# A sliding-window copy: twelve staged batches in 32 KB packets instead of eleven in 16 KB packets

## The chip, the cores and the metric

The kernel runs on one core of one Trainium2 chip. Times are device microseconds of that core, medians of several executions. Nearly all of the work is done by the core's 16 DMA engines, which copy between the main memory (HBM) and the on-chip memory (SBUF), or within HBM; the compute engines only issue transfers. Ratios compare runs of the same chip and the same rounds.

## The reference

The reference cuts each of 32 batches of 4096 rows of 256 float32 into 127 windows of 64 rows, 32 rows apart:

```python
batch, length, dim = (32, 4096, 256)
window_size, stride = 64, 32
for i in range(n_windows):                 # 127
    start = i * stride
    result[:, i] = x[:, start:start + window_size].copy()
```

A block of 32 rows is 32 KB. A window is two neighbouring blocks (64 KB), so every inner block is written twice: as the second half of one window and the first half of the next. The input is 134 MB, the output 266 MB.

## The kernel before

A batch is copied in one of two ways. A direct batch goes from HBM to HBM: each window is read and written, 8.3 MB read and 8.3 MB written. A staged batch is loaded once into an SBUF tile of 128 blocks (4.2 MB) and stored from there twice, once as the first halves and once as the second halves. It reads only 4.2 MB of HBM, but the DMA engines move 4.2 + 8.4 = 12.6 MB for it, where a direct batch moves 8.3 MB.

Three queues run side by side. The scalar engine's queue (q10) issues loads and stores of the staged batches in two groups: loads of six tiles, stores of six, loads of five, stores of five. The sync engine's queue (q1) issues the direct copies. The GpSimd queue (q0) issues the remainders at the end: 127 windows are seven times 16 plus 15, and the 15 next to a staged batch have to wait until that batch is stored, since its stores spill over the edge.

```python
DIRECT, IN, OUT = 32768, 16384, 16384        # bytes of a packet

def windows(self, q, b, w0, n, half=None, piece=DIRECT):     # direct: n windows, whole or one half
    blk = self.blk
    row = [1, 2 * blk if half is None else blk]
    h = half or 0
    return q.dma_start(
        out=self.oap((b * self.nw + w0) * 2 + h, [[2 * blk, n], row]),
        in_=self.xap(b * self.nb + w0 + h, [[blk, n], row]),
        max_dma_last_dim=piece,
    )
# ... Staging:
    parts = [(k, 4, 32, 1) for k in range(4)] if g == 0 else [(0, step, n, step)]   # loads: one DMA a tile
    parts, end = [((0, step, n, step), 0), ((0, step, n, step), 1)], []             # stores: one DMA a half
# ... kernel:
    staged = [*range(1, B, 3)]                                # 11 batches
    share += 120 if turns < 16 or -8 <= second < 16 else 90 if loading else 18
    if share >= 120:                                          # 16 windows as two half-window DMAs
        count(c.windows(ring_d, b, w, 16, 0), done)
        count(c.windows(ring_d, b, w, 16, 1), sem)
    else:                                                     # or as one whole-window DMA
        count(c.windows(ring_d, b, w, 16), sem)
# ... remainders, in groups of 15 windows, on the GpSimd queue:
    ring_r.wait_ge(near, 16)
    for b, w, n in edges:
        ...
        count(c.windows(ring_r, b, w, n), rest)
```

Each DMA on q1 and q10 ends, on every engine that it uses, with a 4-byte semaphore packet, which tells that the data has landed (q1: 204 DMAs, 3264 such packets). In the packet records of the stores (150 to 400 us) the queue changes from one packet of an engine to the next in 99% of the cases, whether data or semaphore packet: the queues take turns, and the semaphore packet takes a turn too. So the number of data packets per semaphore packet in a queue sets how the engine's time is divided. I call the part of the moved bytes that belongs to direct copies (q1 and q0) the direct share.

## Time and profile before

751.6 us (751.08 to 752.81). The page of the kernel before: busy DMA engines in 40 slices, what they moved, and its share by queue.

```profile
span 749.4 us, 322 instructions
DMA  8999999999999999999999999999999999999996
GB/s 360 401 427 429 427 429 428 434 423 418 420 424 423 418 424 415 422 427 427 414 427 417 429 432 429 430 422 430 429 423 421 423 421 419 425 426 423 431 409 262
DMA packets 18290, 313.26 MB, mean 418 GB/s; under 512 B 4336, under 2 KB 4336, under 8 KB 4528
q1 hardware_dynamic: 8016, 154.32, 48.8%
q10 hardware_dynamic: 9104, 138.41, 44.0%
q0 software_dynamic: 1168, 20.51, 6.5%
HBM read 220.95 MB, written 267.09 MB: 651 GB/s over the span
```

The engines are busy from start to end, so every us of this kernel is on the critical path: the chain of waits says nothing more here. The 4336 smallest packets are the semaphore packets.

The stretches view of the kernel before, in the first load phase, first store phase, second load phase, second store phase and the phase of the remainders. Columns: stretch, length, GpSimd busy with its instructions, clock, DMA share, GB/s.

```profile
40.00:125.00 85.00, 0.00 (x0) 1.00 1.01 428
150.00:400.00 250.00, 0.00 (x0) 1.00 1.00 422
420.00:505.00 85.00, 0.00 (x0) 1.00 1.00 429
530.00:650.00 120.00, 0.00 (x0) 1.00 1.01 422
670.00:735.00 65.00, 2.30 (x4) 1.00 1.00 418
```

The rate differs by phase although the engines are never idle. A busy engine is therefore not always at its best; packets take longer in some phases.

The DMA issues of the kernel before (count, KB each, median us from issue to landing) show the forms: whole-window direct DMAs of 1 MB, half-window ones of 512 KB, stores and loads of 4 MB, and remainders of 15 windows.

```profile
out_dram<-in_x_dram SPq DMA_DIRECT2D x92, 1024.0 KB, 100.7
out_dram<-xb ACTq DMA_DIRECT2D x21, 4096.0 KB, 139.7
out_dram<-in_x_dram SPq DMA_DIRECT2D x110, 512.0 KB, 90.3
xb<-in_x_dram ACTq DMA_DIRECT2D x10, 4096.0 KB, 131.4
out_dram<-in_x_dram POOLq DMA_DIRECT2D x20, 960.0 KB, 38.5
```

The trace holds a record of each packet. At best a 32 KB packet takes 1213 ns, a 16 KB packet 611, a 4 KB packet 159 and a semaphore packet 9 (a few records are 2 or 3 ns shorter). Three words follow from these and are used below:

- the floor of a kernel is the sum of the best durations of all its packets over 16 engines;
- the stretch is what the recorded durations have above the floor, in us per engine or in ns per 32 KB (not to be taken for the stretches view, which is the profile's table of pieces of time);
- the lag is how long, on average, an engine has ended its last packet before the last engine ends.

These three are read from one profiled execution of each kernel, while the times are medians; the profiled one can be the fastest of its runs (even12) or the slowest (eleven3).

### The profile page before, as it was taken

What the parts mean: (1) busy time and instruction counts of PE and PEld (TensorE: products, weight loads), DVE (VectorE), ACT (ScalarE), POOL (GpSimd) and SP (SyncE); (2) the same over time, 40 slices, a digit from 0 to 9 for tenths busy, and PEclk for the clock granted to TensorE, in tenths of its full rate; (3) what the DMA queues carried; (4) which work ended last, traced back from release to release, by engine and by line L of the source; (5) the groups of instructions that cost most, each with busy time, mean ns of one, the idle gap of its engine ahead of it and who ended that gap; (6) DMA issues with size and microseconds to landing.
All of it is one profiled execution on the core that took longest, in us unless ns stands there. A gap on an engine that the chain in (4) does not pass through costs nothing.

```text
span 749.4 us, 322 instructions
## 1 busy us (share of the span) xinstructions
POOL 12.8 (2%) x26
## 2 busy tenths in 40 slices
POOL 0000000000000000000000000000000000040100
DMA  8999999999999999999999999999999999999996
GB/s 360 401 427 429 427 429 428 434 423 418 420 424 423 418 424 415 422 427 427 414 427 417 429 432 429 430 422 430 429 423 421 423 421 419 425 426 423 431 409 262
DMA packets 18290, 313.26 MB, mean 418 GB/s; under 512 B 4336, under 2 KB 4336, under 8 KB 4528
## 3 DMA queue, kind: packets, MB, share of 16 engines
q1 hardware_dynamic: 8016, 154.32, 48.8%
q10 hardware_dynamic: 9104, 138.41, 44.0%
q0 software_dynamic: 1168, 20.51, 6.5%
q14 instruction: 2, 0.02, 0.0%
HBM read 220.95 MB, written 267.09 MB: 651 GB/s over the span
## 4 chain that ended last, share of the span: by engine, by line
another core or an unknown queue 92%; POOL 2%; issue 0%; POOLq 0%; SPq 0%
POOL out_dram L34 2%; POOL out_dram L44 0%; POOLq L236 0%; SPq L172 0%; POOLq L114 0%
## 5 line engine op out<-in xcount | busy, mean ns | idle before, releaser
L34 POOL DMA_DIRECT2D out_dram<-in_x_dram x21 | 12.0, 576 | 691.3 <-DMA out_dram<-in_x_dram 654.0
L44 POOL DMA_DIRECT2D out_dram<-in_x_dram x1 | 0.6, 581 | 0.0
L222 POOL MEMSET const-float32-0.0<- 128x1 f32 x1 | 0.1, 98 | 0.2 <-issue 0.2
L222 POOL MEMSET const-bfloat16-1.0<- 128x1 bf16 x1 | 0.1, 101 | 0.0
L222 POOL MEMSET const-float32-1.0<- 128x1 f32 x1 | 0.1, 98 | 0.0
L222 POOL MEMSET const-uint8-127<- 128x1 uint8 x1 | 0.1, 98 | 0.0
## 6 DMA issues: line engine op xcount, KB each, us to landing
out_dram<-in_x_dram SPq DMA_DIRECT2D x92, 1024.0 KB, 100.7
out_dram<-xb ACTq DMA_DIRECT2D x21, 4096.0 KB, 139.7
out_dram<-in_x_dram SPq DMA_DIRECT2D x110, 512.0 KB, 90.3
xb<-in_x_dram ACTq DMA_DIRECT2D x10, 4096.0 KB, 131.4
out_dram<-in_x_dram POOLq DMA_DIRECT2D x20, 960.0 KB, 38.5
xb<-in_x_dram ACTq DMA_DIRECT2D x4, 1024.0 KB, 15.7
out_dram<-xb ACTq DMA_DIRECT2D x2, 1024.0 KB, 113.4
out_dram<-xb ACTq DMA_DIRECT2D x4, 512.0 KB, 96.9
```

Source lines behind the costliest of these rows:

```text
L34: return q.dma_start(out=self.oap((b * self.nw + w0) * 2 + h, [[2 * blk, n], row]), in_=self.xap(b * self.nb + w0 + h, [[blk, n], row]), m ...
L44: return q.dma_start(out=self.oap((b * self.nw + w0) * 2, [[part, 16], [2 * self.blk, n], row]), in_=self.xap(b * self.nb + w0, [[part, 16 ...
L222: nc = _bacc.Bacc("TRN2", target_bir_lowering=False, num_devices=1)
```

## The change

The intent: stage one batch more, which takes load from HBM; move the staged bytes in 32 KB packets like the direct ones, which saves the fixed part of half of the packets; cut loads and stores into as many DMAs as give the wanted direct share; and issue the direct copies in large half-window DMAs with seven packets per engine. The remainders stay last.

```diff
-DIRECT, IN, OUT = 32768, 16384, 16384
+DIRECT, IN, OUT, REST = 32768, 32768, 32768, 32768
+    def many(self, q, b, w0, n, half):
+        return q.dma_start(
+            out=self.oap((b * self.nw + w0) * 2 + half, [[2 * self.blk, 16], [32 * self.blk, n], [1, self.blk]]),
+            in_=self.xap(b * self.nb + w0 + half, [[self.blk, 16], [16 * self.blk, n], [1, self.blk]]),
+        )
 # Staging.load
-        parts = [(k, 4, 32, 1) for k in range(4)] if g == 0 else [(0, step, n, step)]
+        for rows in self.split(2 if g < 6 else 3):
+    def split(self, parts):
+        if parts == 3:
+            return [(0, 4, 32, 1), (2, 4, 32, 1), (1, 2, 64, 1)]
+        return [(k, parts, 128 // parts, 1) for k in range(parts)]
 # Staging.store
+        split = self.split(4 if g >= len(self.items) - 2 else 3)
+        parts, end = [(rows, half) for half in (0, 1) for rows in split], []
 # kernel
-    staged = [*range(1, B, 3)]
+    staged = [0, 3, 6, 9, 11, 14, 17, 20, 22, 25, 28, 31]
+        main += [(b, w + 16 * j, min(7, 7 - j), half) for j in range(0, 7, 7) for half in (0, 1)]
+            edges += [(b, 0, 8), (b, 120, 7)]          # a direct batch between two staged ones
+            edges.append((b, 0 if before else 112, 15))
-        for i, (b, w) in enumerate(sixteens):
-            ...
+        for i, (b, w, n, half) in enumerate(main):
+            count(c.many(ring_d, b, w, n, half), near if i == len(main) - 2 else done)
```

More of the change, by code (lines that the diff above doesn't have):

```diff
@@ L37, in windows, with quarters @@
             max_dma_last_dim=piece,
+        )
+    def quarters(self, q, b, w0, p0, n):
+        part = self.blk // 4
+        at = p0 * 2 * part
+        dims = [[n * part, 2], [1, n * part]]
+        return q.dma_start(
+            out=bass.AP(self.out.tensor, self.oap((b * self.nw + w0) * 2, dims).offset + at, [[2 * self.blk, 4], *dims]),
+            in_=bass.AP(self.x.tensor, self.xap(b * self.nb + w0, dims).offset + at, [[self.blk, 4], *dims]),
+            max_dma_last_dim=4 * n * part,
+        )
+    def many(self, q, b, w0, n, half):
+        return q.dma_start(
+            out=self.oap((b * self.nw + w0) * 2 + half, [[2 * self.blk, 16], [32 * self.blk, n], [1, self.blk]]),
+            in_=self.xap(b * self.nb + w0 + half, [[self.blk, 16], [16 * self.blk, n], [1, self.blk]]),
         )
@@ L87, in load @@
         i = g % len(self.tiles)
-        b, c, n = self.items[g]
         if self.count[self.stored[i]]:
             q.wait_ge(self.stored[i], self.count[self.stored[i]])
-        step = 128 // n
-        parts = [(k, 4, 32, 1) for k in range(4)] if g == 0 else [(0, step, n, step)]
-        for rows in parts:
-            self.issue(self.c.load(q, self.tiles[i], b, c, rows), self.loaded[i])
+        for rows in self.split(2 if g < 6 else 3):
+            self.issue(self.c.load(q, self.tiles[i], *self.items[g], rows), self.loaded[i])
         self.after_load[g] = self.count[self.loaded[i]]
+    def split(self, parts):
+        if parts == 3:
+            return [(0, 4, 32, 1), (2, 4, 32, 1), (1, 2, 64, 1)]
+        return [(k, parts, 128 // parts, 1) for k in range(parts)]
     def store(self, q, g):
         i = g % len(self.tiles)
-        b, c, n = self.items[g]
         q.wait_ge(self.loaded[i], self.after_load[g])
-        step = 128 // n
-        parts, end = [((0, step, n, step), 0), ((0, step, n, step), 1)], []
+        split = self.split(4 if g >= len(self.items) - 2 else 3)
+        parts, end = [(rows, half) for half in (0, 1) for rows in split], []
         if g == len(self.items) - 1:
-            parts = [((0, 1, 128, 1), 1), ((0, 1, 32, 1), 0)]
-            end = [(96, 1, 32, 1)] + [(32 + k, 4, 16, 1) for k in range(4)]
+            parts = [(rows, 1) for rows in split] + [(split[0], 0)]
+            end = split[1:]
         for rows, half in parts:
-            self.issue(self.c.store(q, self.tiles[i], b, c, rows, half), self.stored[i])
+            self.issue(self.c.store(q, self.tiles[i], *self.items[g], rows, half), self.stored[i])
         for rows in end:
-            self.issue(self.c.store(q, self.tiles[i], b, c, rows, 0), self.ended)
+            self.issue(self.c.store(q, self.tiles[i], *self.items[g], rows, 0), self.ended)
         self.after_store[g] = self.count[self.stored[i]]
@@ L140 @@
     c = Copier(x, out, B, L, D, W, S, n_win)
-    staged = [*range(1, B, 3)]
-    items = [(b, -1 if b == B - 1 else 0, c.nb) for b in staged]
-    place = {b: g for g, (b, _, n) in enumerate(items) if n == c.nb}
+    staged = [0, 3, 6, 9, 11, 14, 17, 20, 22, 25, 28, 31]
+    items = [(b, 1 if b == 0 else -1 if b == B - 1 else 0) for b in staged]
+    place = {b: g for g, b in enumerate(staged)}
     direct = [b for b in range(B) if b not in staged]
@@ L157, in count @@
         total[sem] += 16
-    sixteens = []
+    main, edges, singles = [], [], [(B - 1, c.nw - 1, 1)]
+    if 0 in staged:
+        singles.append((0, 0, 0))
+    last = B - 2
     for b in direct:
-        w = 15 if b - 1 in staged else 0
-        sixteens += [(b, w + 16 * j) for j in range((c.nw - w) // 16)]
-    singles = [(B - 1, c.nw - 1, 1)]
-    edges = [(b, 0 if b - 1 in staged else 112, 15) for b in direct[:-1]]
-    last = B - 2
-    edges.append((last, 112, 4))
-    first_loads, loads, stores = 6 * 17, 5 * 17, 6 * 34
-    turns = share = 0
+        before, behind = b - 1 in staged, b + 1 in staged
+        w = 15 if before and (not behind or b == last) else 8 if before else 0
+        if b == last:
+            w = 0
+        main += [(b, w + 16 * j, min(7, 7 - j), half) for j in range(0, 7, 7) for half in (0, 1)]
+        if b == last:
+            edges.append((b, 112, 13))
+        elif before and behind:
+            edges += [(b, 0, 8), (b, 120, 7)]
+        else:
+            edges.append((b, 0 if before else 112, 15))
+    b, w, n, half = main.pop()
+    main += [(b, w, n - 1, half), (b, w + 16 * (n - 1), 1, half)]
     with tc.tile_critical():
         st.run(ring_s)
-        for i, (b, w) in enumerate(sixteens):
-            sem = near if i == len(sixteens) - 2 else done
-            second = turns - first_loads - stores
-            loading = turns < first_loads or 0 <= second < loads
-            share += 120 if turns < 16 or -8 <= second < 16 else 90 if loading else 18
-            if share >= 120:
-                share -= 120
-                turns += 4
-                count(c.windows(ring_d, b, w, 16, 0), done)
-                count(c.windows(ring_d, b, w, 16, 1), sem)
-            else:
-                turns += 3
-                count(c.windows(ring_d, b, w, 16), sem)
-            if i == len(sixteens) // 2:
+        for i, (b, w, n, half) in enumerate(main):
+            count(c.many(ring_d, b, w, n, half), near if i == len(main) - 2 else done)
+            if i == len(main) // 2:
                 for b, w, half in singles:
@@ L196 @@
                     st.wait_stored(ring_r, place[k])
-            count(c.windows(ring_r, b, w, n), rest)
-        count(c.columns(ring_r, last, 116, 9), rest)
+            count(c.windows(ring_r, b, w, n, None, REST), rest)
         st.wait_stored(ring_d, place[B - 1])
```

## The prediction

> **What bounds it now.** Nothing computes; 16 DMA engines copy. The page's slices show DMA at 9 tenths from slice 2 to 39, mean 418 GB/s; part 3 gives q1, q10 and q0 together 99.3% of the engines' time. The stretches view gives 428 to 430 GB/s in the load phases (us 40 to 130 and 425 to 505) and 421 to 423 in the store phases (160 to 285, 300 to 400, 520 to 645), 401 in us 20 to 40, and a falling tail after 740.
>
> From the trace's packet records: a 32 KB packet takes 1213 ns at best and 1236 on average; two 16 KB packets take 1222 at best and 1249 on average; a 4-byte semaphore packet takes 9 ns. The best packet means 432 GB/s over 16 engines, near the 435 of the Trainium skill ("DMA: Bandwidth & Descriptors", Where 436 GB/s comes from). So packet rate is the floor. Above it lies about 17 us of stretched packets, mostly in store phases: 5-us pieces with a direct share (bytes) near 0.59 have 1245 to 1250 ns per 32 KB, near 0.51 only 1220 to 1230. HBM traffic there is about 660 GB/s, so I take the stretch for HBM pressure: a direct packet touches HBM twice, a staged one once.
>
> **What changes.** 11 staged batches become 12. A direct batch moves 8.3 MB through the engines, a staged one 12.5 MB, so DMA bytes rise from 313.3 to about 317 MB: +7 to 8 us at the best rate (plus 1%). HBM traffic falls from 488 to about 484 MB (minus 1%). Staged packets of 32 KB instead of 16 KB save 9 ns per 32 KB (2.4 us per engine), and semaphore packets fall from 271 to about 170 per engine (1 us). The two rings alternate packet by packet (the skill, same page, Queues, rings and completion order; the shares in the trace fit it), so turns set the direct share: 7/8 against 4/5 makes .522 in loads, against 8/11 makes .546 in stores, where before has about .53 and .57.
>
> **The sum.** Floor by an alternating-ring count: before 728 us, after about 734.5. Stretch: before 17; after, loads 1, the start 3, stores at .546 about 1% of 490 us, 5: 9. Ends: 5 us idle plus 2 us between span and time, unchanged. 734.5 + 9 + 7 = 750; if all-half windows also lower the stretch, 746. The direct ring should finish some 10 us before the staged one, which then runs alone at full rate: no loss.
>
> All of it is critical, since the engines never idle; the larger byte count and the smaller stretch nearly cancel.
>
> **Prediction: 748.5 us, 8 in 10 between 742.5 and 755. Faster by over 2%: 0.02, within 2%: 0.95, slower: 0.03.** Faster by 2% means 736.6 us, below the floor plus the ends.
>
> **What would show each step.** DMA bytes about 317 MB, HBM about 217 MB read. Store phases at 425 to 430 GB/s instead of 422, load phases at 430 to 431. q1 with q0 ending before q10. If stores stay at 422 the share was not the cause of the stretch and the time is 755 or more; if they reach 431, 745.
>
> **What would make it wrong.** The stretch belongs to the store's access pattern, not to the HBM sum; the rings drift out of balance, leaving direct packets alone at the end; the windows on the GpSimd ring (298 instead of 304, no multiple of 16) or the final two-window copy leave engines uneven, a few us.

## The result

761.79 us (760.36 to 765.83, 6 runs) against 752.35 us (751.08 to 752.89, 6 runs) on the same chip: ratio 1.0137, 95% interval 1.011 to 1.0163. A ratio is the mean time of one kernel's runs over that of the other's runs of the same rounds, so it is not quite the ratio of the medians. Executions over 1.5% slower than the fastest of the same kernel are left out of the means. The change made the kernel 1.4% slower, and the time lies outside the predicted range of 742.5 to 755.

The page of the changed kernel:

```profile
span 760.1 us, 231 instructions
DMA  8999999999999999999999999999999999999995
GB/s 364 431 421 428 433 426 419 431 433 422 431 421 431 426 428 426 424 431 431 421 402 433 421 421 426 422 417 433 419 428 424 422 428 428 429 410 407 416 405 241
DMA packets 12609, 317.54 MB, mean 418 GB/s; under 512 B 2860, under 2 KB 2860, under 8 KB 2924
q10 hardware_dynamic: 6304, 151.00, 47.2%
q1 hardware_dynamic: 5248, 147.00, 45.6%
q0 software_dynamic: 1056, 19.53, 6.3%
HBM read 216.86 MB, written 267.19 MB: 637 GB/s over the span
```

The bytes are as predicted (317.5 MB through the engines, 216.9 MB read). The mean rate has not moved: 418 GB/s before and after. So 1.4% more bytes took 1.4% more time.

The stretches view of the changed kernel, in its five phases:

```profile
40.00:120.00 80.00, 0.00 (x0) 1.00 1.01 428
140.00:370.00 230.00, 0.00 (x0) 1.00 1.00 427
390.00:505.00 115.00, 0.00 (x0) 1.00 1.00 423
530.00:640.00 110.00, 0.00 (x0) 1.00 1.00 425
670.00:740.00 70.00, 2.88 (x5) 1.00 1.00 408
```

The stores did get faster, from 422 to 427 and 425 GB/s. But the second load phase fell from 429 to 423, and the phase of the remainders from 418 to 408. The DMA issues of the changed kernel show the new forms; note that 18 loads are of 2 MB and 12 of 1 MB, the latter from the second group, which is cut in three:

```profile
out_dram<-in_x_dram SPq DMA_DIRECT2D x39, 3584.0 KB, 167.4
out_dram<-xb ACTq DMA_DIRECT2D x56, 1024.0 KB, 140.1
xb<-in_x_dram ACTq DMA_DIRECT2D x18, 2048.0 KB, 94.5
out_dram<-in_x_dram POOLq DMA_DIRECT2D x17, 960.0 KB, 45.4
xb<-in_x_dram ACTq DMA_DIRECT2D x12, 1024.0 KB, 144.5
```

The packet records give an account that adds up to the span (us per engine; the phases are cut where the staged bytes of each group end, and where the first remainder starts):

```
                                   before   after
floor (best durations)              729.6   736.3
overlap of neighbouring packets      -4.0    -2.5
stretch                              15.0    16.6
   first loads   (direct share)       3.0     3.0     (.537 / .517)
   first stores                       6.3     3.4     (.572 / .539)
   second loads                       0.7     3.7     (.525 / .547)
   second stores, until remainders    2.8     2.1     (.560 / .519)
   remainders                         2.2     4.5     (.584 / .475)
lag at the end                        2.7     3.8
start, last landing                   6.2     5.9
span                                749.4   760.1
```

The overlap row was news to me: with the records of one engine put in a chain (a record does not name its engine, so the chains are inferred from the times), each packet starts about 3.6 ns before the end of the one ahead of it. So, by this reckoning, a saved packet saves 3.6 ns less than its record says.

Of the difference of 10.7 us, 6.7 are the floor, 1.5 the overlap, 1.6 the stretch and 1.1 the lag. The relief of HBM did come in the stores (3.6 us less stretch in both store phases together), but the second loads gave back 3.0 us and the remainders 2.3. Packets that took less than 150 ns too long fell from 9.4 us to 4.9; those that took 300 ns and more too long rose from 78 packets (2.3 us) to 226 (8.3 us).

### The profile page after: what moved, and what is told of

It is laid out like the page before. It is cut to its first block, busy times and chain, and to the rows that moved or that the text cites. A ratio compares the mean times of both kernels' runs of the same rounds, so it can differ in the third digit from the quotient of the medians.

```text
span 760.1 us, 231 instructions
## 1 busy us (share of the span) xinstructions
POOL 12.9 (2%) x26
## 4 chain that ended last, share of the span: by engine, by line
another core or an unknown queue 93%; POOL 2%; issue 0%; POOLq 0%; SPq 0%
POOL out_dram L34 2%; POOLq L252 0%; SPq L201 0%; POOLq L134 0%
```

## The experiments

### First four: the loads, the last stores, eleven batches, and the layouts by themselves

Theory A is that the cut of the staged DMAs into strided rows stalls packets. Its rivals are the direct share, and the remainders.

load2way: `for rows in self.split(2 if g < 6 else 3)` becomes `for rows in self.split(2)`.

> The changed kernel with one edit: the second group of loads is issued in two DMAs per tile like the first, not in three. In the changed kernel the second load phase lost 3.65 us per engine to stretched packets, of which most in packets that took over 300 ns too long; the kernel before lost 0.67 us there. Theory A (the three-way split of the loads causes the long stalls): the second load phase falls to about 1 us of stretch and the time by about 3 us, to 758 to 759. Rival B (the direct share of .547 in this phase, or the addresses met at that time): with B by share, it falls too, since the share goes to .522; with B by addresses or by the transition itself, the stalls stay at over 2.5 us and the time stays at 761 to 762.

Measured: 761.0 us, ratio 1.0106 (1.0082 to 1.013). The stretch of the second loads fell from 3.65 us to 1.30, at a share of .525. The total stretch fell only by 1.0 us, since more direct work was left for the end: 4.85 us of stretch in the remainders and a lag of 4.6 us. The local effect came out as expected; this run does not tell the cut from the share.

tail3: `split = self.split(4 if g >= len(self.items) - 2 else 3)` becomes `split = self.split(3)`.

> The changed kernel with one edit: the last two tiles are stored in three DMAs per half, not in four. The changed kernel lost 4.5 us per engine to stretched packets in the phase of the remainders, plus 4 us of engines ending unevenly. Theory A (the store split in DMAs of two rows per engine stalls): stretch in that phase falls to about 2.5 us, time 2 us lower at most, since the staged ring then also ends earlier and leaves the remainders alone. Rival B (the remainders on the GpSimd ring cause the stalls whatever the split): no change within 1 us, or slower by 1 to 2 us because the staged share rises and the remainders end later.

Measured: 762.19 us, ratio 1.0129 (1.0111 to 1.0148); stretch in the remainders 4.6 us. The cut of the last stores is not the cause there: rival B.

eleven: the staged list of before, its remainders, loads in two and three DMAs, stores in four, in the second group eight:

```diff
-    staged = [0, 3, 6, 9, 11, 14, 17, 20, 22, 25, 28, 31]
+    staged = [*range(1, B, 3)]
-        split = self.split(4 if g >= len(self.items) - 2 else 3)
+        split = self.split(4 if g < 6 else 8)
```

> The changed kernel's packets and direct DMAs (32 KB, 7 windows halves per engine and DMA), but with the eleven staged batches of before and its last remainders, and more splits (loads 2 and 3 DMAs, stores 4, then 8) so that the direct share stays at what eleven batches need. Theory A (the twelfth batch is what costs: 4.2 MB more through the engines, floor 6.7 us higher): the floor is about 726 us, the stretch like before's 15 us or less, the time 747 to 751, so at or under the kernel before. Rival B (the new packets and DMAs cost by themselves): 755 or more.

Measured: 765.18 us, ratio 1.0171 (1.0149 to 1.0194). The floor was 726.8 us as expected, but the stretch 27.3 us, of which 11.5 in the second stores, where stores in eight let the direct share rise to .61. I had missed the share, so this run tells only that too high a share is costly.

layouts: Its output is wrong, which doesn't matter for the time. It runs loads, then stores, in 1, 2, 3 and 4 DMAs per tile with barriers between, first alone and then beside direct DMAs, then stores beside remainders:

```python
for kind, parts, n, other, m in PHASES:       # e.g. ('load', 3, 4, 'many', 5)
    for i in range(n): ...                    # n tiles, each in `parts` DMAs, on the scalar queue
    for j in range(m): ...                    # m direct DMAs on the sync queue, or remainders on GpSimd
    barrier()
```

> A kernel that is wrong on purpose: 21 phases with barriers between them. Each of 1, 2, 3 and 4 DMAs per tile, for loads and for stores, first alone, then beside direct DMAs; then stores in 1, 3 and 4 beside 15-window remainders from GpSimd; then direct DMAs alone and remainders alone. Read from the packet records: mean excess over 1213 ns of each phase. Theory A (layout): three- and four-way splits show long stalls (mean excess over 40 ns) even alone, one- and two-way under 15. Rival B (meeting of streams): no split stalls alone; all splits alike beside direct packets, 10 to 30 ns. Rival C (remainders): the stalls come only in the phases with remainders and even where these run alone.

Measured, over 50 us in the middle of each phase, with the direct share and the sum of HBM bytes read and written per second:

```
                          GB/s   share   HBM GB/s   stretch per 32 KB
loads alone, 1 to 4 DMAs                             0 ns
stores alone, 1 to 4 DMAs                            5 to 7 ns
loads  1 + direct         432.5  .500    649         2 ns
loads  2 + direct         428.3  .510    647        14 ns
loads  3 + direct         418.8  .549    649        40 ns
loads  4 + direct         412.0  .577    650        61 ns
stores 1 + direct         431.5  .506    650         5 ns
stores 2 + direct         430.1  .516    652         7 ns
stores 3 + direct         426.8  .557    665        18 ns
stores 4 + direct         420.4  .574    662        36 ns
stores 1 + remainders     414.6  .407    583        53 ns
stores 3 + remainders     419.4  .455    610        36 ns
stores 4 + remainders     419.2  .488    624        35 ns
direct alone              327.3 1.000    655       390 ns
```

Two lines of the stretches view of this kernel, direct DMAs alone and 15-window remainders alone, show the limit without any arithmetic: the engines stay busy, but the rate is 320 and 326 GB/s.

```profile
1114.00:1144.00 30.00, 0.00 (x0) 1.00 0.98 320
1161.00:1191.00 30.00, 0.00 (x0) 1.00 1.02 326
```

No cut stalls alone, so theory A in its plain form falls. So does rival B, which had all cuts alike: beside direct DMAs the stretch grows with the share, and the HBM sum stays at 647 to 665 GB/s whatever the cut. The exception is the remainders: 35 to 53 ns at HBM sums of only 583 to 624, uncut stores included.

### Share against number of DMAs, and which ring makes the remainders stall

streams: Its output is wrong, which doesn't matter for the time. Loads in four DMAs meet direct DMAs of two packets per engine, which lowers the share to about .49; unsplit loads in 16 KB packets meet direct DMAs of seven packets, which raises it to .65.

> A kernel that is wrong on purpose: 16 phases with barriers. Theory H (the stretch is set by the direct share alone, through HBM: rate = about 657 GB/s over 1 plus the direct share, or the engines' 432 GB/s, whichever is less): loads in four DMAs beside direct DMAs of two packets per engine (share .50) show under 10 ns of mean excess, although four-way loads showed 50 ns at share .577; one-DMA loads in 16 KB packets beside direct DMAs of seven packets (share about .64) fall to about 400 GB/s although they are not split; stores in four beside pairs (.50) under 20 ns. Rival S (the number of splits or DMAs sets it): the four-way phases keep 40 ns and more, the one-DMA phase stays at 425 GB/s or more. Remainders: if the GpSimd ring is the cause of the late stalls, full 16-window DMAs from GpSimd beside three-way stores stall (over 40 ns) and the same from the sync ring do not (under 20 ns); if it is the 15 of 16 engines, only the 15-window ones do; if it is the whole 64 KB windows, both rings do and the half-window ones do not. Direct alone: all near 330 GB/s; if whole windows save HBM effort over half windows, they are some per cent faster alone, and stores in 16 KB packets beside whole windows beat those beside half-window pairs.

Measured, in the stretches view of this kernel (four-DMA loads at a share of .485, then unsplit loads at .648):

```profile
12.00:62.00 50.00, 0.00 (x0) 1.00 1.00 431
97.00:147.00 50.00, 0.00 (x0) 1.00 1.01 400
```

The four-DMA loads have 2.7 ns of stretch where they had 61 at .577, four-DMA stores 1.2; the unsplit loads fall to 400 GB/s at an HBM sum of 657. Theory H holds and rival S falls. (This chip is a faster one than that of layouts: before takes 744.75 us on it. So 61 against 2.7 is not of one chip; four-DMA loads at full rate against unsplit loads at 400 GB/s is.) Half windows and whole windows are equally fast alone (331 GB/s each). The phases on the GpSimd ring issued no direct DMA, by a mistake in my kernel, and were repeated:

streams2: the same, with whole windows in DMAs of 16 or 15, from GpSimd and from the sync ring, beside three-DMA stores.

> Wrong on purpose: the phases for the remainders again (in the earlier trial those from the GpSimd ring issued nothing, by a mistake of mine). Stores in three DMAs of 32 KB packets beside whole windows. If the GpSimd ring causes the long stalls: 16-window DMAs from GpSimd give over 30 ns of mean excess, from the sync ring under 5 (the earlier trial: 1.6). If the 15 of 16 engines cause it: only the 15-window ones, from GpSimd and from the sync ring alike, exceed 30 ns. Half-window pairs from the sync ring repeat about 20. With 16 KB store packets beside 15-window remainders from GpSimd: if packet size matters, few packets over 300 ns too long, at HBM traffic of 658 GB/s; if not, as many as with 32 KB.

Measured, in the stretches view: 16 windows from GpSimd, 15 from GpSimd, 15 from the sync ring, 16 from the sync ring.

```profile
34.00:84.00 50.00, 0.00 (x0) 1.00 1.01 433
123.00:173.00 50.00, 0.00 (x0) 1.00 1.00 417
298.00:348.00 50.00, 0.00 (x0) 1.00 0.99 419
387.00:437.00 50.00, 0.00 (x0) 1.00 1.01 435
```

In the packet records of the same stretches: 0.8 ns of stretch with 16 windows from GpSimd, 40.5 with 15; from the sync ring 1.4 with 16, 14.9 with 15. The long stalls (300 ns and more) number 0, 32, 15 and 0. The ring alone is not the cause, since 16 windows run undisturbed from both; the count of 15 windows is. The ring matters for the size: I had expected over 30 ns from both, and the sync ring has half of that, which no run explains. The Trainium skill ("DMA: Bandwidth & Descriptors", Why a DMA increments its semaphore by 16 and not by 1) says that a DMA runs on the largest number of engines up to 16 that divides its outer dimension, so 15 windows run on 15 (with an exception for some copies from GpSimd); from the sync ring the chains of packet records agree: in these 50 us one engine has 3 direct packets, the others 17 to 20. From GpSimd all sixteen have 18 or 19, so there no engine stays without direct work for long, and the stall is not a matter of lasting uneven load. How 15 windows stall the engines is not shown. Two more readings: beside loads, 15 windows cost nothing (0.0 ns), and beside stores in 16 KB packets, 15 and 16 windows stretch alike (47 and 51 ns over a slightly longer stretch, at shares of .57 and .59, where the HBM limit is reached). So the 15 windows are seen to matter only beside stores in 32 KB packets; with 16 KB packets the HBM limit may hide what they add. Each phase of stores beside direct DMAs also begins with some 24 to 48 packets stalled by over 150 ns in its first 10 us, whatever the DMAs, and then runs nearly without any where all engines get the same work and the share is under .5; I read this as the engines falling into step, which an uneven DMA breaks again. That reading is argued, not shown.

### Putting the finds into the kernel

eleven2 takes eleven batches with shares nearer to before's; even12 keeps twelve and evens the share out.

```diff
 # eleven2: loads split(2), stores split(4), the last three tiles in 16 KB packets
+        piece = OUT if g < 8 else OUT // 2
 # even12: loads split(2)
+        split = self.split(1 if g >= 9 else 3 if g % 2 else 2)
+        piece = OUT if g < 9 else OUT // 2
```

> Eleven staged batches again, with 32 KB packets and seven-half direct DMAs, but now with the direct shares that the kernel before had: loads in two DMAs, stores in four (about .57), the last three tiles in four DMAs of 16 KB packets beside the remainders (about .58). The first trial with eleven failed since its stores in eight had a share of .61 and ran into the HBM limit (11 us of stretch in one phase). Theory A (the twelfth batch and the uneven shares are what costs, the packets are a small gain): floor 727 us, stretch 13 to 16, time 747 to 752, the same as the kernel before or 0.5% under it. Rival B (32 KB packets or half-window direct DMAs cost by themselves): 755 or more.

Measured: 760.31 us where the kernel before took 755.62 on this chip; ratio 1.0068 (1.0035 to 1.0102). The stretch was 24.9 us. In the second stores the share was .59 again, since the 16 KB tiles came up while the main part still ran. A miss, by my own sizing.

> The changed kernel with twelve batches but the direct share held nearer to one value: loads in two DMAs (.522), stores in three and two by turns (about .535), the last three tiles unsplit in 16 KB packets so that the remainders get about .54 instead of .475. Theory A (the loss lies in shares over .53 in loads and stores and in the remainders beside 32 KB stores): stretch falls from 16.6 to about 11 us, the uneven end from 4 to 3, the time to 752 to 756. Rival B (the remainders' long stalls stay whatever the staged packets): stretch in that phase stays over 4 us and the time at 757 or more.

Measured: 759.73 us, ratio 1.006 (1.0029 to 1.0092), less than half of the changed kernel's loss, though that was measured on another chip. The stretch fell to 11.4 us, with 1.3 in the remainders (share .52, stores in 16 KB packets) and 1.4 in the second loads; the lag was 2.5 us. The stretch and the lag came out as theory A said, the median 4 us over its range, on a chip where before itself was 3 us slower. The profiled execution (755.45 us) was the fastest of the four; what the others lost above it no trace shows.

### One chip for all: before, after, even remainders, and the best of twelve

> The kernel before, for a profile on the same chip as the next three runs, since the trials showed that chips differ in what their HBM gives. Expected: 15 us of stretched packets per engine if this chip is like the first one, over 18 if its time is over 755.

Measured: 744.02 us, stretch 7.6 us (a single look, so its state is unknown; the seven timed runs of before on this chip have a median of 744.6). This chip has half of the stretch of the first one with the same kernel.

> The changed kernel once more, for the same reason and for the ratio to before on this chip. Expected ratio 1.01 to 1.016, 16 to 18 us of stretch, over 4 us of it in the phase of the remainders.

Measured: 756.48 us, ratio 1.0159 (1.0134 to 1.0184), stretch 9.0 us. My expectation for the stretch was taken from the slower chip and missed, but the account of the difference is the same: floor 6.7, stretch 1.5, overlap 1.5, lag 0.4 us.

edge16 issues the remainders as 16 windows, one of them written a second time after the first write has landed:

```diff
-            edges += [(b, 0, 8), (b, 120, 7)]
+            edges += [(b, 0, 16), (b, 111, 16)]      # with 96 windows, not 112, in the main part of such a batch
-            edges.append((b, 0 if before else 112, 15))
+            edges.append((b, 0 if before else 111, 16))
+        ring_r.wait_ge(body, total[body])            # all main DMAs but the last two
```

> The changed kernel, with its remainders in DMAs of 16 windows, not 15, 8 or 7, so that all 16 engines get the same work: one window is written twice, after the first write has landed, with the same bytes (1.3 MB more, about 2.9 us of floor). Theory (remainders on 15 of 16 engines beside stores cause the long stalls; seen in the trials with barriers: 35 to 47 ns of mean excess against 1 to 2): stretch in that phase falls from 4.5 to under 2 us and the uneven end from 4 to about 3; the time is 0 to 3 us lower in spite of the added bytes. Rival (something else in that phase, such as the store split or the waits of GpSimd): stretch stays over 4 us and the time rises by 3 us.

Measured: 754.07 us, ratio 1.0122 (1.0105 to 1.0139), 2.4 us less than the changed kernel although the floor is 2.8 us higher. This gain is not clear of the noise: the two intervals overlap, and of the two profiled executions edge16's is 1.0 us the slower. The stretch in the remainders fell from 3.3 us to 0.5, and the packets there that took 300 ns and more too long from 65 to 13; even12, with 15 windows beside stores in 16 KB packets, has 1. The stretches view of the remainders in the changed kernel on this chip:

```profile
660.00:735.00 75.00, 2.88 (x5) 1.00 1.00 414
```

The same view of edge16:

```profile
650.00:735.00 85.00, 2.57 (x5) 1.00 1.00 431
```

With streams2 this makes 15-window DMAs beside 32 KB stores the cause of most of the long stalls in the remainders. The lag did not fall (4.9 us), which the theory had got wrong.

best12 adds loads in two DMAs, stores in three and two by turns, and the last three tiles in four.

> The 16-window remainders together with loads in two DMAs throughout and stores in three and two by turns, the last three tiles in four: the direct share is held at .50 to .535 everywhere. If the three terms found (share over .53 in the loads, share in the stores, remainders on 15 engines) are the whole of the loss beyond the bytes, stretch falls to 8 to 10 us; floor 739; time 1.000 to 1.006 of before, so a tie and no gain, because the twelfth batch and the doubled windows cost 10 us of floor.

Measured: 754.95 us, ratio 1.0145 (1.0124 to 1.0165). The stretch was 5.9 us, and in the second loads 0.1: the stretches view has them at the engines' best.

```profile
380.00:485.00 105.00, 0.00 (x0) 1.00 1.00 433
```

But the expected tie did not come. On this chip before loses only 7.6 us to stretch, so there were not 10 us to win; the floor of 739.0 us decides. The remainders on q0 also ended 9 us after the staged queue.

### Do the packets and the direct DMAs cost anything by themselves?

eleven3: eleven batches, loads in three, stores in four, only the last two tiles in 16 KB packets; before_third is the kernel before on the same chip.

> The kernel before, for its profile on the chip of the next run: floor 729.6 us, stretch between 7 and 19 us, as its time on this chip tells.

> Eleven staged batches with 32 KB packets and half-window direct DMAs, now with loads in three (.546) and stores in four (.567) and only the last two tiles in 16 KB packets, so that the share stays under .57 while the main part runs (the second trial had .59 there). If the new packets and DMAs cost nothing by themselves: floor 727 us, stretch within 2 us of before's on this chip, ratio to before .995 to 1.004. If they cost by themselves: stretch over 4 us above before's and ratio over 1.006.

Measured: before 753.56 us with 17.2 us of stretch; eleven3 761.78 us, ratio 1.0072 (1.0041 to 1.0103), with 28.4 us of stretch. The floor was 726.8 us. At first loads of equal share (.54) it had 4.9 us against 2.8, and in the second stores, at .541 against .560, 6.0 against 3.4. Part of the gap in stretch is the choice of executions (eleven3's profiled one is the slowest of its four, before's single one is at the fast end), but the ratio is over 1 although the floor is 2.8 us lower. So something does cost by itself, and the share is not the whole law. Two runs take the parts one by one.

before32 is the kernel before with 32 KB staged packets, in eight DMAs per tile so that a turn still moves 16 KB on average; halfpairs is the kernel before with most whole-window direct DMAs replaced by pairs of half-window ones.

```diff
 # before32
-DIRECT, IN, OUT = 32768, 16384, 16384
+DIRECT, IN, OUT = 32768, 32768, 32768
+        parts = [(k, 8, 16, 1) for k in range(8)]        # loads; stores likewise
-            share += 120 if ... else 90 if loading else 18
+            share += 120 if ... else 65 if loading else 0
 # halfpairs, for two neighbouring groups of 16 windows
-                count(c.windows(ring_d, b, w, 16), sem)
+                    count(c.many(ring_d, b, w - 16, 2, 0), done)
+                    count(c.many(ring_d, b, w - 16, 2, 1), done)
```

> The kernel before with one thing changed: the staged packets are 32 KB, in DMAs of one packet per engine (eight per tile), so that the staged ring's turn moves 16 KB on average as it did with 16 KB packets, and the direct share stays about the same (.57 in stores; the mixture of direct DMAs is shifted a little to keep it). Eleven batches, whole windows, remainders as before. If the 32 KB staged packets by themselves bring the long stalls that the third trial with eleven batches showed: stretch over 5 us above before's 17 on such a chip, and a ratio over 1.005. If the packets are innocent: floor 2 us lower, stretch about the same, ratio .994 to 1.002.

> The kernel before with one thing changed: most whole-window direct DMAs (two 32 KB packets of one window per engine) become pairs of half-window DMAs (two packets of two windows 16 apart), with the same count of packets and turns, so the same shares. Staged packets stay at 16 KB. If half-window direct DMAs cost by themselves (a block is read again only later): stretch over 5 us above before's and a ratio over 1.005. If they are innocent: ratio .997 to 1.003.

Measured: halfpairs 745.89 us, ratio 1.0012 (0.9996 to 1.0029), so half-window DMAs in pairs are innocent; in sevens they were not tried alone. before32 gave 765 to 790 us in four runs, where before gave 745.3; two of the four count as slow, so no ratio is drawn from it. The stretches view of its profiled (fast) run, in the first loads and the first stores:

```profile
10.00:90.00 80.00, 0.00 (x0) 1.00 1.00 340
150.00:400.00 250.00, 0.00 (x0) 1.00 1.01 428
```

Its stores, in eight DMAs of 32 KB packets, ran as fast as before's on a chip of like speed (before_again, 150 to 400 us: 428 GB/s too), and as fast as those of halfpairs on the same chip (426 there, and 425 against 424 in the second stores). So 32 KB packets in stores are innocent at this share. Its remainders are not: 15 windows beside 32 KB stores, 73 packets stalled by 300 ns and more, where halfpairs with 16 KB stores has 1. Its first loads stalled for 20.9 us per engine, at a share of .527 and an HBM sum of 510 to 535 GB/s, and recovered after 100 us by themselves. Loads that are finely cut can stall for a reason that is not the HBM sum.

load3share asks this of the changed kernel itself: the three-DMA loads stay, and the direct DMAs that meet them are cut in two, which lowers the share.

```diff
+    main = [(b, w + 16 * a, k, half) for i, (b, w, n, half) in enumerate(main)
+            for a, k in (((0, 4), (4, 3)) if 23 <= i < 32 else ((0, 7),))]
```

> The changed kernel again, for its profile on the chip of the next run. Second load phase at a share of .547: 1.6 us of stretch on a fast chip (as in after_again), 3.6 on a slow one.

> The changed kernel with its three-DMA loads kept, but the direct DMAs that meet the second group of loads cut in two (four packets and three per engine, so 7 data packets in 9 turns), which takes the direct share there from .547 to about .517, as far down as the two-DMA loads took it. If the share sets the stretch of the loads: the second load phase falls to under half of the control's (1.3 us or less where the control has 3.6; 0.8 or less where it has 1.6). If the splitting of the loads sets it, as before32's 21 us in its first load phase suggests: it stays within 30% of the control's.

Measured: the control after_third took 757.7 us, with 2.0 us of stretch in the second loads at .547; load3share has 0.4 us there at .501. The stretches view of the second loads in the control:

```profile
390.00:505.00 115.00, 0.00 (x0) 1.00 1.00 429
```

The same view of load3share:

```profile
390.00:490.00 100.00, 0.00 (x0) 1.00 1.01 433
```

So in the changed kernel it was the share, not the cut of the loads (one profile each; the direct DMAs were also shorter). The time did not follow: 758.35 us, ratio 1.015 (1.0093 to 1.0207; the four runs spread from 751.8 to 761.0). What the direct queue did not move in the second loads had to be moved later: the remainders began at 654 us, not 648, and finished 9 us after the staged queue (3 in the control), with a lag of 8.1 us.

No version beat the kernel before.

## Why the prediction was wrong

The prediction said 748.5 us; 761.8 was measured. Its sum was 734.5 of floor, 9 of stretch and 7 of ends. Measured: 736.3, 16.6 and 9.0 (overlap, lag, start and landing, and the 1.8 us between span and time). The headline of 748.5 was also 1.5 us under its own sum, for a hope that half windows would lower the stretch; halfpairs shows that they don't.

- "DMA bytes rise ... plus 7 to 8 us at the best rate", with a floor from 728 to 734.5: right. The floor rose by 6.7 us, and that is most of the loss. The level was 1.8 us too low.
- "Staged packets of 32 KB instead of 16 KB save 9 ns per 32 KB": too high. Because neighbouring packets overlap by 3.6 ns, a saved packet is worth about 5.4 ns. This is the 1.5 us in the overlap row.
- "Stores at .546 about 1% of 490 us, 5": right until the remainders began. Both store phases together had 5.5 us. In mid-phase (530 to 640 us) the share was .545 as forecast. That the stretch follows the direct share, with a nearly constant HBM sum, was shown by layouts and streams, and for the loads by load3share; eleven3 shows that the share is not all.
- "After, loads 1, the start 3": here a step failed. I took ".522 in loads" for all loads. The second group is cut in three, and by the same count of turns that makes .546, which was measured as .547. These loads had 3.7 us where before had 0.7. With the two-DMA cut it was 1.3, and with the three-DMA cut at a share of .501 it was 0.4 against 2.0 for the control.
- The remainders had no term of their own. I had only listed uneven engines as a risk of "a few us". They took 4.5 us of stretch at an HBM sum of about 600 GB/s, where the share law allows none, because 15-window DMAs beside 32 KB stores stall; with 16 windows 0.5 us remained of 3.3.
- "The direct ring should finish some 10 us before the staged one": it did not. The remainders on q0 ended at 756.7 us, the staged queue at 754.0 (before: 745.8 and 745.2).
- "Ends: ... unchanged": the lag grew by 1.1 us on the first chip. How much of this belongs to the 15 windows is open: edge16 did not lower it.
- "Stores ... if they reach 431, 745; if they stay at 422 ... 755 or more": they reached 425 to 427, and the time was still over 755. The store rate was not the only test that this sum needed.

So the step that failed is the stretch term: predicted to fall from 17 to 9 us, it went from 15.0 to 16.6. HBM relief did what it should in the stores, and 3.6 us of it were given back as 5.3 us in the second loads and the remainders. That left the added bytes unpaid.

Two things stay open. Why eleven3 stretches more than the kernel before at nearly equal shares: half windows in pairs and 32 KB stores were cleared one by one, but not their combination, nor half windows in sevens, nor the cut of the loads at shares over .53. And why the first loads of before32 stalled for 100 us and then recovered.

## What to carry to other kernels

Where a kernel trades bytes through the DMA engines against bytes through HBM, write one sum for each of the two limits and for each phase: a phase pays the larger one, and a good average share does not help a phase that is over the limit. Whatever share is taken out of one phase comes back in another, most often at the end, so look there first when a local gain doesn't reach the time. And give every DMA an outer count that is a multiple of 16: uneven DMAs cost nothing beside loads here, but 15 to 40 ns on each 1213 ns packet beside stores in 32 KB packets.

## What the Trainium skill lacked or had wrong

- "DMA: Bandwidth & Descriptors", Where 436 GB/s comes from: its 435 GB/s agrees (432 by the best packet). Under Latency and other measured facts the page has copies between HBM tensors at up to 214 GB/s per direction; direct copies here moved more, 319 to 331 GB/s, so 638 to 662 GB/s read and written together, and a mixed load is held to about 650 to 671. "HBM Reference", Specifications, sees a core streaming alone as bounded by its 16 engines at about 425; direct copies alone stay far below that, at about the HBM sum at which mixed loads stop too, so I take HBM for their bound.
- "DMA: Bandwidth & Descriptors", Queues, rings and completion order: turns by packet fit the measured shares, to about .02, only if the 4-byte semaphore packet counts as a turn of its own, which the page doesn't say. With seven data packets against four it gives .522, and .510 to .525 were measured; with the three-way cut .546, and .539 to .557.
- The same page, How many engines: that 15 windows use 15 engines agrees for the sync ring. No page says that such a DMA can slow the other queue: 40.5 ns per packet beside 32 KB stores, 0.0 beside loads. Nor does the count of semaphore packets fit, if all 4-byte packets are such: 22 remainder DMAs left 460 of them on q0 instead of the 352 that 16 per DMA make, and 358 when nearly all had 16 windows.
- No page mentions the differences between chips: the kernel before took 744.6 us on one and 755.7 on another, with 7.6 and 17.2 us of stretch.
- "DMA: Bandwidth & Descriptors", Two DMAs through the same engine are not ordered, says that the descriptors of a queue are pipelined, but no page says by how much packets of one engine overlap: 3.6 ns here.
